# Where a two-layer transformer kernel puts its modulation work, how its first stream's norm is split, and how its first two query heads are ordered

## The chip, the cores and the metric

The kernel runs on one core of one Trainium2 chip. The metric is the device time of one execution in microseconds (us), lower is better. The core has TensorE (PE in the profile; PEld are its weight loads), VectorE (DVE), ScalarE (ACT), GpSimd (POOL) and SyncE (SP, which here only issues DMAs). Each engine works through its own queue in order; they wait for one another through semaphores. The instruction order on each engine comes from the framework's planner, which places instructions by their dependences and by where the program issues them.

## The reference

Two streams of 256 tokens with 1024 features go through two layers: `lat` (the first stream, s = 0) and `cx`, the context (the second stream, s = 1). Each layer has a feed-forward net (SwiGLU, 2816 hidden features), a mixer and a second feed-forward net. Each of the three steps is preceded by an RMS norm that is modulated, and its result is added through a gate. The nine shift, scale and gate vectors of a layer come from a product of the condition with a 1024 x 9216 matrix.

```python
mod  = (silu(c) @ mod_w[i] + mod_b[i]).reshape(bsz, 3, 3, 1, 1024)
modc = (silu(c_ctx) @ mod_w[i] + mod_b[i]).reshape(3, 3, 1024)
_modulate(t, g, shift, scale) = rms(t) * g * (1 + scale) + shift
lat = lat + 0.5 * mod[:,0,2] * swiglu(modulate(lat, norm_g[i,0], mod[:,0,0], mod[:,0,1]))   # cx likewise
lat = lat + mod[:,1,2] * mixer(...)       # layer 0: gated 3-tap convolution; layer 1: attention, 8 query and 2 key heads
lat = lat + 0.5 * mod[:,2,2] * swiglu(modulate(lat, ...))   # cx likewise, in layer 0 only
```

Everything is float32; only `lat` is returned.

## The kernel before

**Arithmetic.** x is held transposed: eight tiles (k = 0 to 7) of 128 features x 512 columns, the first stream in columns 0 to 255, the second in 256 to 511. A float32 product is made of three matmuls on a high and a low part (`mm3`, lines 137 to 139): w high by m high, w high by m low, w low by m high. Every weight and every operand is split first: ScalarE makes the high part (`split`, line 108, wh, bh, gh), VectorE the low part as the difference (line 109, wl, bl, gl).

**Stages in order.** `ffn(0, 0)`, the convolution's input product, its output product `cw_out`, `ffn(0, 1)`, `ffn(1, 0)`, attention, `wo` and `ffn(1, 1)` (that last one has only the first stream left). A feed-forward net for both streams runs in three parts (THIRDS: 8, 7 and 7 tiles of hidden features). Each part is a stretch of *block pairs* and then a *product* (`project`) of the hidden tiles with w2 into x.

**Block pairs.** `Pair` (lines 693 to 777) computes gate and up of one hidden tile in the seven-product form for 2 x 2 blocks: sums of weight blocks (VectorE lines 728 and 736, GpSimd line 706 with an adding DMA at 709, and a split w4h on ScalarE at 113 with w4l behind it) and then products in two PSUM tiles p and q (`head`, `five`, `six`, `seven`, `four`). Line 759 copies q into gm on ScalarE between two products into q.

**Products.** `project` (lines 586 to 645) makes eight output tiles m. The first `nf` (two or three) are interleaved with the end of the pairs; then one tile after another. `finish` adds the gated result into x on VectorE (line 569). A product that is followed by a norm (the third of a net, and `cw_out`) has `late` = 2: its tiles 6 and 7 are done at the end per stream and per half of the hidden tiles, so that the norm of the first stream can begin while the second stream's tiles are still computed.

**Norm.** `square_add` squares x on ScalarE (line 264, sq) and adds up on VectorE (line 272, acc). `rms_sum` adds over partitions with one-column matmuls (line 281, ss), takes the root on ScalarE (line 287) and the reciprocal on VectorE (line 290); `rms_all` spreads it with matmuls (line 299). Then each k tile is scaled on VectorE (line 311, t), shifted on ScalarE into the high part and made into the low part on VectorE. `Plain` does the latter two per k tile (lines 321 and 322). `Blocks` keeps four k tiles of one K half in one 128 x 1024 tile per stream, and a raw copy (line 405, hr). With `fine` it writes the high part (line 400, bh) and the low part (line 401, bl) per k tile; without, one `split` of the whole 128 x 1024 tile follows (lines 407, 108, 109). `fine` is set for the first stream's first K half only.

**Modulation.** After the first two chunks, the modulation's product isn't done on TensorE. One *unit* is a multiply-and-reduce on VectorE of 128 rows of the matrix with the condition (line 179, junk, and a readout of the accumulator into mod). The matrix rows (in_modT) come through SP's queue into the same ring of eight raw buffers (wr) as the weights. Units are handed out by `tick(n)`: it adds n to what is owed and issues whole units. There are ticks after product tiles (line 622 for the first nf, line 633 for the others up to tile 5, or up to tile 4 where late = 2), one of 0.5 in each pair (line 841), 5 for each tile of the convolution, and a few in attention. `ev` is the number for a product's tile: one value for the first two products of a net, one for its third. With `at` (late = 2 and m > 2) the units are placed behind that tile's line-569 instruction. `gate_of` and `mod_ready` issue at once whatever unit is needed and still missing.

**Attention.** `q_proj(p)` makes two query heads (i = 0, 1) side by side in one PSUM tile, all k of the first and then all k of the second. `sums` squares them on ScalarE and adds up over partitions; `rotate` scales them on ScalarE and applies the rotary tables.

Of the kernel before, what the change touches and what calls it, by code (L numbers as in the profile page):

```python
# [12 lines left out]
AF = mybir.ActivationFunctionType  # L13
# [34 lines left out]
def hybrid_kernel(ctx: ExitStack, tc: tile.TileContext, a: dict, out: bass.AP):  # L48
# [471 lines left out]
    def tail_norm(l, j, h):  # L520

        box = {}

        def tail(m, c0, c1):
            square_add(m, c0, c1)
            if m == KT - 1:
                if not box:
                    box["A"] = scale_of(l, j)
                    box["B"] = mod_ready(l, 3 * j)
                s = c0 // S  # L530

                def inv():
                    return rms_inv(s, (accs[s], accs[s, "last"]))

                def rest(part, ri):

                    if isinstance(h, Blocks):
                        h.block(s, part, box["A"], box["B"], ri, fine=s == 0 and part == 0)
                    else:
                        for k in range(4 * part, 4 * part + 4):  # L540
                            norm_k(s, k, h, box["A"], box["B"], ri)

                def both_parts():
                    ri = inv()
                    for part in range(2):
                        rest(part, ri)

                if s == 0:
                    keep = []

                    def one():
                        keep.append(inv())
                        rest(0, keep[0])

                    pending.append(one)
                    pending.append(lambda: rest(1, keep[0]))
                else:
                    flush()
                    pending.append(both_parts)

        return tail
# [24 lines left out]
    def project(ws, src, nk, gate, tail, tot, late, ev, between=()):  # L586

        def products(ps, w, ks, c0, c1, wide=True):
            ms = [src(k, c0, c1) for k in ks]
            if wide and len(ms[0]) == 3:
                return mm_wide(ps, [w(k) for k in ks], ms, ks[0] == 0, ks[-1] == nk - 1)
            for k, m in zip(ks, ms):
                mm3(ps[:, : c1 - c0], w(k), m[:2], k == 0, k == nk - 1)

        nf = 3 if between else 2  # L600
        ahead = {}

        def get(m):
            for i in range(m, min(m + 3, KT)):
                if i not in ahead:
                    ahead[i] = ws(i)
            return ahead[m]

        w2 = [get(m) for m in range(nf)]
        p2 = [psum("py") for _ in range(nf)]  # L610
        cut = nk - 2 if between else nk - 1
        for i in range(nf):
            products(p2[i], w2[i], range(cut), 0, tot)
            if i < len(between):
                between[i]()
        if between:
            for i in range(nf):
                products(p2[i], w2[i], (nk - 2,), 0, tot)
        for i in range(nf):
            products(p2[i], w2[i], (nk - 1,), 0, tot)  # L620
            finish(i, p2[i], 0, tot, gate, tail, len(src(0, 0, tot)) == 3)
            tick(ev)

        for m in range(nf, KT - late):
            if tail and tot == S and m == KT - 2:
                ready()
            w = get(m)
            ps = psum("py")
            wide = len(src(0, 0, tot)) == 3 and m < KT - 1
            products(ps, w, range(nk), 0, tot, wide)  # L630
            ins = finish(m, ps, 0, tot, gate, tail, wide)
            if m < (5 if late else 6):
                tick(ev, ins if late and m > 2 else None)
        if late:

            wl = [get(m) for m in (6, 7)]
            if tail:
                ready()
            for s in range(2):
                for i in range(2):  # L640
                    ps = psum("py")
                    products(ps, wl[i], range(nk // 2), s * S, s * S + S)
                    flush(1)
                    products(ps, wl[i], range(nk // 2, nk), s * S, s * S + S)
                    finish(6 + i, ps, s * S, s * S + S, gate, tail)
# [133 lines left out]
    def ffn(l, b, h, tot, gate, tail, gs=(), ev=(0, 0), z=None):  # L779
        gs = list(gs)  # L780
        i0 = 0
        for t, n in enumerate(THIRDS):
            between = ()
            if tot == T2:
# [23 lines left out]
                for i in range(len(gs), n):  # L808
                    if t == 0 and not heads and i in AS_IS[l, b]:
                        w = load_w(a["w13"][l, b, i])  # L810
                        pp = psum("pg"), psum("pu")
                        if prev:
                            prev.seven()
                        if "T1" not in h.t:
                            with tc.issue_after(rows["W1"]):
                                h.sums()
                        w13_mm(pp, w, h, range(4), 0, T2)
                        if prev:
                            gs.append(new_pair("g"))
                            prev.four(gs[-1])  # L820
                            prev = None
                        w13_mm(pp, w, h, range(4, KT), 0, T2)
                        gs.append(new_pair("g"))
                        tick(3, w13_post(pp, gs[-1], 0, T2))
                        continue
                    if heads:
                        pr = heads.pop(0)
                    else:
                        pr = Pair(a["w13"][l, b, i0 + i], h)
                        pr.sums(0)  # L830
                        pr.sums(1)
                        pr.head()
                    pr.five()
                    if prev:
                        prev.seven()
                    pr.six()
                    if prev:
                        gs.append(new_pair("g"))
                        prev.four(gs[-1])
                    prev = pr  # L840
                    tick(0.5)

                def last():
                    gs.append(new_pair("g"))
# [231 lines left out]


    hn = Plain()
    ffn(0, 0, h, T2, gate_of(0, 0), tail_norm(0, 1, hn), gs0, (2.9, 2.4))
    h = hn  # L1080

    zs = []
# [37 lines left out]
    def by_pairs(key, box=None):  # L1120
# [10 lines left out]
    hn = Blocks()  # L1131
    project(
        by_pairs("cw_out"), lambda k, c0, c1: (zs[k][0][:, c0:c1], zs[k][1][:, c0:c1]), KT,
        gate_of(0, 1), tail_norm(0, 2, hn), T2, 2, 1.8,
    )
    h = hn
    hn = Blocks()
    ffn(0, 1, h, T2, gate_of(0, 2), tail_norm(1, 0, hn), (), (2.7, 2))
    h = hn


    hn = Plain()
    ffn(1, 0, h, T2, gate_of(1, 0), tail_norm(1, 1, hn), (), (2.5, 1.6))
    h = hn
    ap = ctx.enter_context(tc.tile_pool(name="ap", bufs=2))

# [2 lines left out]

    def sums(ps, c):  # L1150
        sq = tp.tile([P, T2], F32, name=nm("sq"), tag="gm", bufs=3)
        nc.scalar.activation(out=sq, in_=ps, func=AF.Square)
        for i in range(4):
            nc.tensor.matmul(
                pqs[:, c + i : c + i + 1], sq[:, i * P : i * P + P], ones[:, 0:1],
                start=True, stop=True,
            )

    def rotate(ps, gain, n):

        kn = hot("kn", F32)[:, :T2]
        nc.scalar.activation(out=kn, in_=ps, func=AF.Identity, scale=gain)
        rt = tp.tile([P, T2], F32, name=nm("rt"), tag="sg", bufs=3)
        for o in range(0, P, 32):
            nc.scalar.dma_start(rt[o : o + 32, : n * S], kn[o ^ 32 : (o ^ 32) + 32, : n * S])
        v3 = lambda t: t[:, : n * S].rearrange("p (i t) -> p i t", i=n)
        sb = sinT.unsqueeze(1).to_broadcast([P, n, S])
        cb = cosT.unsqueeze(1).to_broadcast([P, n, S])
        nc.vector.tensor_tensor(out=v3(rt), in0=v3(rt), in1=sb, op=ALU.mult)
        kc = tp.tile([P, T2], F32, name=nm("kc"), tag="gm", bufs=3)  # L1170
        nc.vector.tensor_tensor(out=v3(kc), in0=v3(kn), in1=cb, op=ALU.mult)
        nc.vector.tensor_tensor(
            out=kn[:, : n * S], in0=kc[:, : n * S], in1=rt[:, : n * S], op=ALU.add
        )
        return kn

    def q_proj(p):
        wq = load_w(a["wq"][p])
        ps = psum("pq")
        for i in range(2):  # L1180
            for k in range(KT):
                mm3(
                    ps[:, i * S : i * S + S], wq(k * 256 + i * P), pick(h, k, 0, S),
                    k == 0, k == KT - 1,
                )
        return ps

    qs, krs = [], []

# [6 lines left out]
    def k_proj(kv):  # L1196
        ps = psum("pk")
        for k in range(KT):
            mm3(ps, wk(k * 256 + kv * P), pick(h, k, 0, T2), k == 0, k == KT - 1)
        return ps  # L1200

    def k_rope(kv, ps):
        sums(ps, 16 + 4 * kv)
# [272 lines left out]
```

## Time and profile before

| | |
|---|---|
| median of 3 runs | 1571.19 us (1570.63 to 1572.66) |
| profiled execution | 1571.39 us |
| its span, first to last instruction | 1569.6 us |
| mean granted TensorE clock | 0.998 |
| PE busy | 1554.6 us (99%) |
| DVE busy | 1284.9 us (82%) |
| ACT busy | 779.2 us (50%) |
| POOL busy | 224.4 us (14%) |

The profile is that of one execution; times count from the start of its span. A row of a timeline has start, duration, engine, line, operation, what is written and read, and in brackets the idle time ahead of it with what ended it. A row of waits has the waiting engine and what it waited for, then the total, the number of times and the longest. Consecutive PE rows overlap: matmuls are pipelined, so the distance between starts tells the pace, not the duration. The stages lie at: first net 48 to 382 us (its products at 114 to 161, 229 to 270 and 339 to 382), convolution to 516, `cw_out` to 564, `ffn(0, 1)` to 917, `ffn(1, 0)` to 1267, attention to 1358, the rest to 1569.6.

### The profile page before, as it was taken

What the parts mean: (1) busy time and instruction counts of PE and PEld (TensorE: products, weight loads), DVE (VectorE), ACT (ScalarE), POOL (GpSimd) and SP (SyncE); (2) the same over time, 40 slices, a digit from 0 to 9 for tenths busy, and PEclk for the clock granted to TensorE, in tenths of its full rate; (3) what the DMA queues carried; (4) which work ended last, traced back from release to release, by engine and by line L of the source; (5) the groups of instructions that cost most, each with busy time, mean ns of one, the idle gap of its engine ahead of it and who ended that gap; (6) DMA issues with size and microseconds to landing.
All of it is one profiled execution on the core that took longest, in us unless ns stands there. A gap on an engine that the chain in (4) does not pass through costs nothing.

```text
span 1569.6 us, 26355 instructions
## 1 busy us (share of the span) xinstructions
PE 1554.6 (99%) x10282; PEld 1423.0 (91%) x10282; DVE 1284.9 (82%) x2023; ACT 779.2 (50%) x1289; POOL 224.4 (14%) x188
## 2 busy tenths in 40 slices
PE   9999999999999999999999999999999999999999
PEld 7898998999888899989989899989999899898888
DVE  5789789779997688987987798987978797887676
ACT  5642552644423366436346476436345355674553
POOL 0013203200000022041131021031041002300000
PEclk9999999999999999999999999999999999999999
DMA  9567657554564434664664544664765664356562
GB/s 371 190 181 205 146 155 201 120 174 147 181 223 161 129 100 121 195 175 106 199 168 125 166 119 122 195 171 112 254 170 156 195 197 144 97 192 210 171 199 74
DMA packets 88253, 263.53 MB, mean 168 GB/s; under 512 B 10816, under 2 KB 12608, under 8 KB 88128
## 3 DMA queue, kind: packets, MB, share of 16 engines
q1 hardware_dynamic: 69408, 230.72, 45.3%
q0 software_dynamic: 16128, 29.37, 11.1%
q10 hardware_dynamic: 2592, 1.76, 0.4%
q8 instruction: 80, 1.31, 0.3%
q14 instruction: 45, 0.37, 0.1%
HBM read 259.45 MB, written 1.05 MB: 166 GB/s over the span
## 4 chain that ended last, share of the span: by engine, by line
PE 83%; DVE 8%; DMA 4%; issue 2%; ACT 2%; ACTq 0%; POOL 0%; POOLq 0%; DVEq 0%; SPq 0%
PE py L137 7%; PE py L138 7%; PE py L139 7%; PE p L137 6%; PE p L138 6%; PE p L139 6%; PE q L137 5%; PE q L139 5%; PE q L138 5%; DVE junk L179 2%; PE py L145 2%; PE pg L145 2%; PE pu L145 2%; DVE wl L109 2%; DMA wr<-in_w 1%
## 5 line engine op out<-in xcount | busy, mean ns | idle before, releaser
L108 ACT ACTIVATE wh<-wr 128x1024 fp32r<-128x1024 f32 (+2 forms) x446 | 394.6, 913 | 339.3 <-PE py L138 127.1
L109 DVE TENSOR_TENSOR wl<-wr,wh 128x1024 fp32r<-128x1024 f32 (+2 forms) x446 | 458.0, 1051 | 106.5 <-ACT wh L108 84.8
L179 DVE CUSTOM_DVE_ANT_0 junk<-wr,scbc,modb 128x1024 bf16<-128x1024 f32 x222 | 286.0, 1288 | 26.0 <-DMA wr<-in_modT 23.9
L137 PE MATMUL py<-gh,wh 128*128 128x512 f32 (+1 forms) x570 | 213.4, 374 | 0.0
L138 PE MATMUL py<-gl,wh 128*128 128x512 f32 (+1 forms) x570 | 213.3, 374 | 0.0
L139 PE MATMUL py<-gh,wl 128*128 128x512 f32 (+1 forms) x570 | 212.9, 373 | 0.0
L706 POOL TENSOR_SCALAR wr<-wr 128x512 f32<-128x512 f32 x56 | 100.5, 1795 | 714.6 <-DMA wr<-in_w 495.9
L569 DVE SCALAR_TENSOR_TENSOR x<-py,mod,x 128x256 f32<-128x256 f32 x213 | 94.2, 478 | 41.4 <-PE py L139 30.2
L138 PE MATMUL p<-tl,wh 128*128 128x256 f32 x448 | 126.8, 283 | 0.0
L139 PE MATMUL p<-th,wl 128*128 128x256 f32 x448 | 126.8, 283 | 0.0
L137 PE MATMUL p<-th,wh 128*128 128x256 f32 x448 | 126.7, 283 | 0.0
L139 PEld LDWEIGHTS py<-gh,wl 128*128 128x128 f32 x570 | 107.3, 188 | 19.2
L137 PEld LDWEIGHTS py<-gh,wh 128*128 128x128 f32 x570 | 107.4, 188 | 18.3
L138 PEld LDWEIGHTS py<-gl,wh 128*128 128x128 f32 x570 | 107.4, 188 | 18.1
L115 POOL DMA_DIRECT2D w4l<-in_w x56 | 52.0, 929 | 280.8 <-ACT w4l L114 204.9
L137 PE MATMUL q<-bh,wh 128*128 128x256 f32 x320 | 90.8, 284 | 0.7 <-ACT gm L759 0.7
L139 PE MATMUL q<-bh,wl 128*128 128x256 f32 x320 | 90.7, 283 | 0.2 <-DVE wl L109 0.2
L138 PE MATMUL q<-bl,wh 128*128 128x256 f32 x320 | 90.5, 283 | 0.0
L137 PEld LDWEIGHTS p<-th,wh 128*128 128x128 f32 x448 | 86.0, 192 | 0.4
L138 PEld LDWEIGHTS p<-tl,wh 128*128 128x128 f32 x448 | 86.0, 192 | 0.3
L139 PEld LDWEIGHTS p<-th,wl 128*128 128x128 f32 x448 | 86.0, 192 | 0.0
L766 ACT ACTIVATE sg<-sg 128x512 f32<-128x512 f32 x56 | 35.4, 632 | 86.7 <-DVE sg L765 86.6
(304 smaller groups left out, 4067.6 us busy)
## 6 DMA issues: line engine op xcount, KB each, us to landing
wr<-in_modT SPq DMA_DIRECT2D x126, 512.0 KB, 4.9
wr<-in_w SPq DMA_DIRECT2D x120, 512.0 KB, 4.5
wr<-in_w2b SPq DMA_DIRECT2D x64, 448.0 KB, 4.0
wr<-in_w2a SPq DMA_DIRECT2D x32, 512.0 KB, 4.9
wr<-in_w SPq DMA_DIRECT2D x56, 256.0 KB, 4.0
wr<-in_w POOLq DMA_DIRECT2D x56, 256.0 KB, 4.9
w4l<-in_w POOLq DMA_DIRECT2D x56, 256.0 KB, 5.9
pm<-in_mod SPq DMA_DIRECT2D x16, 512.0 KB, 10.2
```

Of the source, the lines that this page charges most:

```text
L108: nc.scalar.activation(out=hi, in_=src, func=AF.Copy)
L109: return nc.vector.tensor_tensor(out=lo, in0=src, in1=hi.bitcast(F32), op=ALU.subtract)
L115: nc.gpsimd.dma_start(out=lo, in_=src, accum_op=ALU.add)
L137: nc.tensor.matmul(ps, wh, mh, start=first, stop=False, **kw)
L138: nc.tensor.matmul(ps, wh, ml, start=False, stop=False, **kw)
L139: nc.tensor.matmul(ps, wl, mh, start=False, stop=last, **kw)
L145: nc.tensor.matmul(ps, w[0], m[2], start=first and n == 0, stop=False)
L179: nc.vector.tensor_tensor_reduce(out=junk, in0=raw[j], in1=scbc[:, v, :], scale=0.5 if ch in (2, 8) else 1.0, scalar=modb[:, l, col : col ...
L569: ins = nc.vector.scalar_tensor_tensor(out=x[:, m, s * S : s * S + S], in0=ps[:, o : o + S], scalar=g[:, m, s : s + 1], in1=x[:, m, s * S ...
L706: nc.gpsimd.tensor_scalar(out=r1[:, :T2], in0=r2[:, :T2], scalar1=-1.0, scalar2=None, op0=ALU.mult)
L766: nc.scalar.activation(out=self.sg, in_=self.sg, func=AF.Silu)
```

## The change

There are four edits.

- `fine` is set for both K halves of the first stream. The second K half's single split of 128 x 1024 (one ScalarE, one VectorE instruction) becomes four of each with 128 x 256. This concerns the norms ahead of `ffn(0, 1)` and `ffn(1, 0)`.
- In a product the tick of the last tile that had one is dropped: tile 5 has none any more where late = 0, tile 4 where late = 2. The numbers `ev` of the remaining ticks go up.
- In the block pairs a tick of 0.8 stands behind every pair but the first of a stretch, in place of 0.5 behind each.
- `q_proj(0)` uses two PSUM tiles, one for each head, and goes through k with both heads at each k. `sums` and `rotate` take a list of tiles; for pair 0 each of their ScalarE instructions becomes two of 256 columns.

```diff
-                        h.block(s, part, box["A"], box["B"], ri, fine=s == 0 and part == 0)
+                        h.block(s, part, box["A"], box["B"], ri, fine=s == 0)
...
-            if m < (5 if late else 6):
-                tick(ev, ins if late and m > 2 else None)
+            if m < 5 - late // 2:
+                tick(ev, ins if late and m == 3 else None)
...
-                    tick(0.5)
+                    if i:
+                        tick(0.8)
...
-    ffn(0, 0, h, T2, gate_of(0, 0), tail_norm(0, 1, hn), gs0, (2.9, 2.4))
+    ffn(0, 0, h, T2, gate_of(0, 0), tail_norm(0, 1, hn), gs0, (3, 2.7))
...
     project(
         by_pairs("cw_out"), lambda k, c0, c1: (zs[k][0][:, c0:c1], zs[k][1][:, c0:c1]), KT,
-        gate_of(0, 1), tail_norm(0, 2, hn), T2, 2, 1.8,
+        gate_of(0, 1), tail_norm(0, 2, hn), T2, 2, 2.2,
     )
...
-    ffn(0, 1, h, T2, gate_of(0, 2), tail_norm(1, 0, hn), (), (2.7, 2))
+    ffn(0, 1, h, T2, gate_of(0, 2), tail_norm(1, 0, hn), (), (2.8, 2.4))
...
-    ffn(1, 0, h, T2, gate_of(1, 0), tail_norm(1, 1, hn), (), (2.5, 1.6))
+    ffn(1, 0, h, T2, gate_of(1, 0), tail_norm(1, 1, hn), (), (2.8, 2))
...
     def sums(ps, c):
         sq = tp.tile([P, T2], F32, name=nm("sq"), tag="gm", bufs=3)
-        nc.scalar.activation(out=sq, in_=ps, func=AF.Square)
+        for o, p in enumerate(ps):
+            n = p.shape[1]
+            nc.scalar.activation(out=sq[:, o * n : o * n + n], in_=p, func=AF.Square)
...
-        nc.scalar.activation(out=kn, in_=ps, func=AF.Identity, scale=gain)
+        for o, p in enumerate(ps):
+            m = p.shape[1]
+            nc.scalar.activation(
+                out=kn[:, o * m : o * m + m], in_=p, func=AF.Identity, scale=gain
+            )
...
     def q_proj(p):
         wq = load_w(a["wq"][p])
-        ps = psum("pq")
-        for i in range(2):
-            for k in range(KT):
-                mm3(
-                    ps[:, i * S : i * S + S], wq(k * 256 + i * P), pick(h, k, 0, S),
-                    k == 0, k == KT - 1,
-                )
-        return ps
+        if p == 0:
+
+            ps = [psum("pq")[:, :S] for _ in range(2)]
+            order = [(i, k) for k in range(KT) for i in range(2)]
+        else:
+            ps = psum("pq")
+            ps = [ps[:, :S], ps[:, S:], ps]
+            order = [(i, k) for i in range(2) for k in range(KT)]
+        for i, k in order:
+            mm3(ps[i], wq(k * 256 + i * P), pick(h, k, 0, S), k == 0, k == KT - 1)
+        return ps[2:] or ps
```

More of the change, by code (lines that the diff above doesn't have):

```diff
@@ L1199, in k_proj @@
             mm3(ps, wk(k * 256 + kv * P), pick(h, k, 0, T2), k == 0, k == KT - 1)
-        return ps
+        return [ps]
     def k_rope(kv, ps):
```

## The prediction

> **What bounds the kernel now.** I read the page's busy shares first, then its slices, then the chain that ended last.
>
> ```profile
> span 1569.6 us, 26355 instructions
> PE 1554.6 (99%) x10282; PEld 1423.0 (91%) x10282; DVE 1284.9 (82%) x2023; ACT 779.2 (50%) x1289; POOL 224.4 (14%) x188
> ...
> PEclk9999999999999999999999999999999999999999
> ...
> PE 83%; DVE 8%; DMA 4%; issue 2%; ACT 2%; ACTq 0%; POOL 0%; POOLq 0%; DVEq 0%; SPq 0%
> ```
>
> TensorE is busy for 99% of the span at nearly full clock, and 83% of the chain is its own work. The change removes no matmul, so it can win only what TensorE loses between matmuls; 1569.6 - 1554.6 = 15.0 us is idle in all. The view of TensorE's waits says for whom it stood still:
>
> ```profile
> PE q L137 <- ACT gm L759: 1.9, 2, 1.2
> PE ss L281 <- ACT sq L264: 1.7, 2, 1.0
> ...
> PE pg L138 <- DVE bl L109: 1.0, 1, 1.0
> PE ss L281 <- DVE acc L272: 0.7, 2, 0.4
> ...
> PE ss L299 <- DVE ri L290: 0.6, 1, 0.6
> ...
> PE pq L137 <- ACT hh L321: 0.4, 1, 0.4
> ...
> PE pv L137 <- ACT hh L321: 0.3, 1, 0.3
> PE pq L138 <- DVE hl L322: 0.3, 1, 0.3
> ```
>
> All of these stand at seams, where one product ends and the next stage begins; the waits inside attention and the start-up are not touched by the edits. They add up to 6.9 us. The tables by stretch show which engine is short there (columns: length, then busy time of PE, PEld, DVE, ACT, POOL, then clock; the last row counts the modulation reductions of line 179 alone):
>
> ```profile
> 228.88:269.91 41.03, 41.03 (x195) 34.42 (x193) 40.10 (x65) 11.92 (x16) 9.47 (x8) 1.00 0.72 213
> 269.91:338.70 68.79, 67.58 (x563) 67.38 (x562) 55.24 (x76) 40.49 (x69) 14.40 (x13) 1.00 0.56 139
> ...
> 559.10:562.60 3.50, 3.50 (x19) 3.50 (x18) 2.35 (x7) 1.68 (x5) 1.93 (x2) 0.51 0.93 193
> ...
> 871.00:917.00 46.00, 44.83 (x261) 39.56 (x260) 35.60 (x67) 20.27 (x32) 7.00 (x7) 1.00 0.56 167
> ...
> 1260.00:1273.00 13.00, 12.07 (x92) 11.14 (x92) 11.96 (x27) 6.83 (x14) 0.00 (x0) 1.00 0.53 183
> ```
> ```profile
> 269.91:338.70 68.79, 6.37 (x10) 1.00 0.56 139
> ```
>
> VectorE is 98% busy in a product (40.10 of 41.03 us) without stopping TensorE, and 80% busy in the block pairs behind it (55.24 of 68.79). What it has not finished when the product ends is what TensorE waits for. One row more: the clock is 0.51 for the one stretch from 559.10.
>
> **The change, part by part.** Durations are those of the profiled execution: 1571.39 us, of which 1569.6 are the span and 1.8 lie around it; it is 0.2 above the median of the runs, 1571.19.
>
> *Ticks off the last tiles (line 632), higher rates, and 0.8 a pair instead of 0.5 (line 841).* In the first ffn a product that took six ticks of 2.9 (17.4 units) takes five of 3 (15 units), so the last tick's three units no longer stand behind tile 5; pairs get six ticks of 0.8 (4.8) instead of seven of 0.5 (3.5). The seam at 275 us:
>
> ```profile
> 275.42 0.28 PE L138 MATMUL p<-tl,wh 128*128 128x256 f32 x1
> 275.54 0.28 PE L139 MATMUL p<-th,wl 128*128 128x256 f32 x1
> 277.03 0.39 PE L137 MATMUL q<-hh,wh 128*128 128x256 f32 x1 [1.21 <-ACT gm L759]
> ```
> ```profile
> 269.85 1.27 DVE L179 CUSTOM_DVE_ANT_0 junk<-wr,scbc,modb 128x1024 bf16<-128x1024 f32 x1
> 271.06 0.08 DVE L179 DVE_READ_ACCUMULATOR2_ANT mod<- 128x1 f32 x1
> ...
> 274.81 0.68 DVE L728 TENSOR_TENSOR wr<-wr 128x512 f32<-128x512 f32 x1
> ```
> ```profile
> 275.66 1.06 ACT L108 ACTIVATE wh<-wr 128x1024 fp32r<-128x1024 f32 x1 [3.75 <-DVE wr L728]
> ```
>
> The matmul waits for the copy gm (line 759), which on ScalarE is queued behind the split wh, which waits for VectorE's line 728. A unit is 1.27 + 0.08 = 1.35 us of VectorE; three gone put line 728 up to 4.0 us earlier, more than the wait. Matmuls start 1.49 us apart here and 0.12 apart before (275.42, 275.54), so the loss is 1.37: a listed wait costs 0.16 more than its entry. The row of waits has two such (1.9 us), so 2.2 us go if all goes; nothing goes if line 728's weights land late instead. I take -1.9, nearer the first, since ScalarE and VectorE, not a DMA, are named in these rows.
>
> The work comes back in the pairs: 1.3 units on average, at most 2, or 2.7 us of VectorE, so 57.9 of 68.79 us (84%). What hides it: 13.5 us of VectorE idleness in that stretch, 1.9 for each of seven pairs. I take 0; the product before it, 98% busy with TensorE full, is the nearest row. Without that cover it is the slow rival below. The modulation loads (512 KB each) move past pair loads on SP's queue too; POOL's loads keep their order. They share the ring of eight raw buffers, so a load can wait there, and what is behind it on SP waits with it.
>
> *No modulation behind the late tiles at 556 us (cw_out; m < 4 instead of m < 5).*
>
> ```profile
> 556.61 0.28 PE L138 MATMUL py<-zl,wh 128*128 128x256 f32 x1
> 557.86 0.38 PE L281 MATMUL ss<-ones,sq 128*128 128x1 f32 x2 [0.97 <-ACT sq L264]
> ...
> 561.22 0.41 PE L137 MATMUL py<-zh,wh 128*128 128x256 f32 x1
> 561.43 0.41 PE L138 MATMUL py<-zl,wh 128*128 128x256 f32 x1
> ```
> ```profile
> 555.67 1.28 DVE L179 CUSTOM_DVE_ANT_0 junk<-wr,scbc,modb 128x1024 bf16<-128x1024 f32 x1
> ...
> 556.88 0.48 DVE L569 SCALAR_TENSOR_TENSOR x<-py,mod,x 128x256 f32<-128x256 f32 x1
> ```
> ```profile
> 554.36 0.63 ACT L113 ACTIVATE w4h<-wr 128x512 fp32r<-128x512 f32 x1 [2.19 <-DMA wr<-in_w]
> ```
>
> The last square waits for x of tile 7, which waited behind a unit (1.28 us from 555.67) on VectorE. That unit is gone in the new order, so the stall of 0.97 + 0.16 = 1.1 goes. Right behind it the clock halves: matmuls 0.21 us apart instead of 0.12. About 15 of the 19 in that stretch are full ones, so 15 x 0.09 = 1.35 us. The other long stalls (1.21 at 275, 0.96 at 924) show no such drop, so that the stall was its cause is likely, not certain. I take both, -2.5; with the ri wait (0.6 + 0.16) it could be -3.2, and 0 if w4h's late load (ScalarE idle 2.19 us for it) still holds the square up.
>
> [...]
>
> *First stream's norm by k tile in the second K half (line 538), with the last tick gone there too.* The seam from 909 to 925:
>
> ```profile
> 924.14 0.28 PE L137 MATMUL pu<-bh,wh 128*128 128x256 f32 x1
> 925.38 0.39 PE L138 MATMUL pg<-bl,wh 128*128 128x256 f32 x1 [0.96 <-DVE bl L109]
> ```
> ```profile
> 915.02 1.26 DVE L311 SCALAR_TENSOR_TENSOR t<-x,A,ss 128x256 f32<-128x256 f32 x3
> 916.25 0.48 DVE L401 SCALAR_TENSOR_TENSOR bl<-t,mod,bh 128x256 fp32r<-128x256 f32 x1
> ...
> 924.11 1.22 DVE L109 TENSOR_TENSOR bl<-hr,bh 128x1024 fp32r<-128x1024 f32 x1
> ```
> ```profile
> 918.09 0.50 ACT L400 ACTIVATE bh<-t,mod 128x256 fp32r<-128x256 f32 x1
> 918.49 0.50 ACT L405 ACTIVATE hr<-t,mod 128x256 f32<-128x256 f32 x1
> ```
>
> One bl of 1.22 us that must be whole becomes four of 0.48, each needed at its own k; TensorE now waits at each, with pu of the same k queued behind. On VectorE four cost 1.92 - 1.22 = 0.7 more, on ScalarE about as much (four of 0.50 for one of 1.06 us: 0.9); ScalarE is busy 20.27 of 46 us there, so this hides. What is late next is VectorE's supply: 0.42 for t and 0.48 for bl, 0.9 us per k tile, against six matmuls of 0.12 = 0.72 on TensorE. Over three tiles that leaves 3 x 0.18 = 0.5 of the wait of 0.96 + 0.16. The waits ss for sq (1.7 - 0.97 = 0.7) and for acc (0.4) stand behind units of the last tick, which go; with 0.16 each they are 1.4, and I take 0.9 for what another load on ScalarE may keep. Together -(0.6 + 0.9) = -1.5; the ends are -2.5 and +0.7 (the added VectorE work, uncovered). The same edit before the first ffn's second half has no listed wait for bl: 0.
>
> *First query heads side by side, and the seams to conv (381 us) and attention (1262 us).* In pair 0 each k tile now feeds two heads, so TensorE takes 0.72 instead of 0.36 us per k while the norm supplies one in about 0.9; the listed waits pq are 0.4 + 0.3, with 0.16 each 1.0, and the table has 13.00 - 12.07 = 0.93 idle. Two 256-column copies replace one of 512 in sums and rotate, ScalarE only (6.83 of 13 busy). I take -0.7, ends -1.0 and +0.4. At conv pv's wait (0.3 + 0.16) loses the units ahead of its norm: -0.4, ends -0.5 and 0.
>
> Sum: -1.9 - 2.5 - 1.5 - 0.7 - 0.4 + 0 = -7.0, so 1571.39 - 7.0 = 1564.4 us. All gains at their ends: -2.2 - 3.2 - 2.5 - 1.0 - 0.5 = -9.4, 1562.0. All at the other end: 0 + 0 + 0.7 + 0.4 + 0 = +1.1, 1572.5.
>
> **The rivals.**
>
> *The waits are handed on* (1569.7 us). ScalarE's strict order keeps the squares behind w4h's load and the weights behind line 728 land late; only half of the waits of q for gm (1.1) and the 0.6 of bl go: -1.7, 1569.7. For it: 2.19 us of ScalarE idleness for a DMA at 552 to 554. Against: the rows nearest the stalls name VectorE's units.
>
> *More goes than the waits show* (1560). Of the 15.0 us idle the rows quoted above are 6.9; the other 8.1 hold start-up and attention, but also stops at the seams too short to be listed, which a VectorE that is ahead would take too. I put this end at the -9.4 and 2 of the 8.1, so -11.4.
>
> *Slower: pairs starve* (1576). A unit whose load is late stops VectorE in order.
>
> ```profile
> DVE junk L179 <- DMA wr<-in_modT: 23.9, 19, 3.8
> ```
>
> It waited 19 times, up to 3.8 us. In a product this is covered by nothing being urgent; in a pair VectorE's room is 1.9 us, and the pair's own splits stand behind. If in the six pair stages after a first product one such wait exceeds the room by its whole 3.8 - 1.9 = 1.9 us, it costs 11.4, and with the gains 1571.39 - 7.0 + 11.4 = 1575.8. It decides from four such waits on (7.6 us). For it: loads sharing one ring with the pair's. Against: pairs already carry five units in 68.79 us and show no wait behind them but the seam's.
>
> *The clock drop stays, or falls elsewhere*, the change doing the rest, because a stop of 1 us is not what halves it: 1564.4 + 1.35 = 1565.8, in the forecast's own range. Against it speaks the place, right behind the stop; for it that two other stops did nothing. [...]
>
> **How the numbers follow.** A chance of 0.50 for the forecast (1561.5 to 1567.5), 0.15 of it for the clock drop that stays, 0.12 for more than the waits show, 0.22 for waits handed on, 0.16 for starving pairs. 0.2% (3.1 us) is about what a measurement of this kernel can tell from no change. Faster takes the forecast and the second case, 0.62; within 0.2% the handed-on waits, 0.22; slower 0.16. The range, 1560 to 1574, leaves out the far half of the slow case and a little of the fast one.
>
> **What the profile after would show.** Right: no row of q waiting for gm at the first seam; no wait of ss for sq near 557, and no stretch of clock near 0.5 there; four bl of 0.48 us in place of 1.22 near 923, with a wait under 0.6; line 179 at about 15 units instead of 17 in a product and about 5 to 6 in a pair stage, TensorE as busy as 67.58 of 68.79 or more there. Wrong: new rows of p or q waiting for wl or wh inside pair stages, modulation waiting longer for its loads than 23.9 us, or the squares still behind w4h.

## The result and the profile after

The changed kernel is slower by a little: median 1573.61 us over 22 executions (1569.73 to 1579.83) against 1570.68 us for the kernel before (1567.11 to 1572.66); the ratio is 1.0023 with a 95% interval of [1.0013, 1.0032]. The forecast was 1564.4 us and faster.

The profiled execution took 1570.84 us, with a span of 1569.1 us and a granted clock of 0.998; it is one of the quicker ones. Over the 22 executions the clock lay between 0.992 and 0.999, mean 0.9964; before's, in the four sets taken for the experiments, had means of 0.9980 to 0.9985. In the profile before, one window at half clock lasts 3.4 us (matmul starts are 0.21 us apart from 559.1 to 562.5). Such a window counts 3.4 x 0.5 / 1570 = 0.0011 of the mean clock, so by this estimate the changed kernel runs through one to two of them more. A line through its 22 points gives 1.2 us for each 0.001: some 2 of the 2.9 us between the medians go along with the clock.

The page after, its busy shares:

```profile
span 1569.1 us, 26378 instructions
PE 1552.7 (99%) x10282; PEld 1421.2 (91%) x10282; DVE 1282.2 (82%) x2029; ACT 776.3 (49%) x1297; POOL 223.0 (14%) x188
```

TensorE idles 1569.1 - 1552.7 = 16.4 us where it idled 15.0. The total hardly moved; the places did. TensorE's waits after:

```profile
PE ss L281 <- DVE acc L272: 3.8, 3, 1.9
PE pq L139 <- DVE wl L109: 3.0, 1, 3.0
PE ss L299 <- DVE ri L290: 1.2, 2, 0.6
...
PE q L137 <- ACT wh L108: 0.4, 1, 0.4
...
PE pg L138 <- DVE bl L401: 0.2, 1, 0.2
```

The waits of q for gm, of ss for sq, of pv and pq for hh are gone, and bl's fell from 1.0 to 0.2. In their place stand acc (0.7 before, 3.8 now) and one of 3.0 us for wl in attention, at a place that had none. Of acc's waits one is at the start-up, which the edits leave alone: 0.32 us of the 0.7 and 1.91 us of the 3.8 (0.2 to 1.9 us over the profiles of all runs here). The two others are new in size: 0.76 at 905 us and 1.10 at 1257. q's wait for wh, 0.39 us, is new, too; it is at 591 us, in the first block pair of `ffn(0, 1)`. TensorE's timeline at the stop in attention, and the clock behind it (after's table by stretch):

```profile
1296.86 1.05 PE L1249 MATMUL kri<-ident,rq 128*128 128x128 f32 x8
1300.93 0.57 PE L139 MATMUL pq<-hh,wl 128*128 128x256 f32 x1 [3.02 <-DVE wl L109]
...
1301.52 0.41 PE L138 MATMUL pq<-hl,wh 128*128 128x256 f32 x1
1301.73 0.41 PE L139 MATMUL pq<-hh,wl 128*128 128x256 f32 x1
```
```profile
1300.80:1304.40 3.60, 3.47 (x16) 3.47 (x17) 3.60 (x6) 0.00 (x0) 0.00 (x0) 0.53 0.75 198
```

The fourth query pair's product stops at its third matmul. Matmul starts are 0.21 us apart behind the stop instead of 0.12; the 14 matmuls until 1304.3 take some 14 x 0.09 = 1.3 us more. What VectorE did meanwhile (timeline after):

```profile
1295.55 0.08 DVE L179 DVE_READ_ACCUMULATOR2_ANT mod<- 128x1 f32 x1
1299.32 0.42 DVE L1176 TENSOR_TENSOR rt<-rt,sinT 128x256 f32<-128x256 f32 x1 [3.68 <-DMA rt<-kn]
1299.66 1.22 DVE L109 TENSOR_TENSOR wl<-wr,wh 128x1024 fp32r<-128x1024 f32 x1
```

It did nothing for 3.68 us: the rotation rt of the second key head waits for its DMAs, and the low part wl that TensorE wants is queued behind it. Before, that low part stood ahead of the rotation (timeline before):

```profile
1299.35 1.22 DVE L109 TENSOR_TENSOR wl<-wr,wh 128x1024 fp32r<-128x1024 f32 x1
...
1303.69 0.43 DVE L1169 TENSOR_TENSOR rt<-rt,sinT 128x256 f32<-128x256 f32 x1 [0.77 <-DMA rt<-kn]
```

### The profile page after: what moved, and what is told of

Its sections match the earlier page's. It is cut to its first block, busy times and chain, and to the rows that moved or that the text cites. A ratio compares the mean times of both kernels' runs of the same rounds, so it can differ in the third digit from the quotient of the medians.

```text
span 1569.1 us, 26378 instructions
## 1 busy us (share of the span) xinstructions
PE 1552.7 (99%) x10282; PEld 1421.2 (91%) x10282; DVE 1282.2 (82%) x2029; ACT 776.3 (49%) x1297; POOL 223.0 (14%) x188
## 4 chain that ended last, share of the span: by engine, by line
PE 89%; DVE 5%; DMA 3%; ACT 2%; issue 1%; ACTq 0%; POOLq 0%; POOL 0%; DVEq 0%; SPq 0%
PE py L138 8%; PE py L137 8%; PE py L139 8%; PE p L137 7%; PE p L138 7%; PE p L139 7%; PE q L139 5%; PE q L137 5%; PE q L138 5%; PE py L145 2%; PE pu L145 2%; PE pg L145 2%; DVE wl L109 1%; PE pv L138 1%; PE pv L137 1%; PE pv L139 1%
## 5 line engine op out<-in xcount | busy, mean ns | idle before, releaser
L179 DVE CUSTOM_DVE_ANT_0 junk<-wr,scbc,modb 128x1024 bf16<-128x1024 f32 x220 | 283.6, 1289 | 37.2 <-DMA wr<-in_modT 35.4
L113 ACT ACTIVATE w4h<-wr 128x512 fp32r<-128x512 f32 x56 | 35.2, 628 | 86.7 <-DMA wr<-in_w 47.9
```

Source lines behind the costliest of these rows:

```text
L113: nc.scalar.activation(out=hi, in_=raw, func=AF.Copy)
L179: nc.vector.tensor_tensor_reduce(out=junk, in0=raw[j], in1=scbc[:, v, :], scale=0.5 if ch in (2, 8) else 1.0, scalar=modb[:, l, col : col ...
```

## The experiments

The first four runs take the change apart.

**The heads one after another again, all else as changed.** The edit gives `q_proj`, `sums` and `rotate` back their old form (of the edit, the loop alone):

```diff
-        if p == 0:
...
-            ps = [psum("pq")[:, :S] for _ in range(2)]
-            order = [(i, k) for k in range(KT) for i in range(2)]
...
+        for i in range(2):
+            for k in range(KT):
...
```

> The changed kernel with the first query heads one after the other again. Theory A (the new order in attention: the low part of the third query weights stands behind a rotation that waits for its DMA; TensorE stops 3.2 us at 1297 us and the clock halves behind it): both go, so the seams' gain of about 7 us shows; about 1564.5, ratio to before 0.9955 to 0.9965. Theory B (the changed kernel's short stops at 566, 590, 904, 1256 halve the clock in one execution and not in another, and that is the loss): only the 3.2 us go, 1569.5 to 1571, and the granted clock of its executions still spreads from 0.992 to 0.999. Theory C (the added modulation in the pairs costs): as B, with TensorE waits in pair stages.

Measured: 1571.58 us, ratio 1.001 [1.0001, 1.0019]. The stop at 1297 us is gone, as A and B had it, but the seams' gain of A doesn't show, and the time is 0.6 us above the range of B: the last seam got worse (2.27 us of waiting for acc at 1258 us), and the clock of the 12 executions lay between 0.996 and 1.0, not down to 0.992.

```profile
PE ss L281 <- DVE acc L272: 4.1, 3, 2.3
...
PE pq L138 <- DVE hl L322: 0.7, 4, 0.2
```

**The side-by-side heads alone on the kernel before.**

> The kernel before with the first query heads side by side and nothing else. Theory A: the attention order is disturbed here too, a stop of 2 to 4 us there and often a halved clock window (1.5 us) behind it: 1572 to 1576. Theories B and C: no more than 1 us from before.

Measured: 1569.17 us, ratio 0.9993 [0.9984, 1.0002]: no cost and no stop in attention. Theory A as stated falls: this edit by itself does not make the stop. Here the first low part of the fourth pair (1298.55) stands ahead of the rotation (1301.68, 0.60 us of waiting); only together with the moved ticks does the planner lay them the other way round. (Whether it needs the norm by k tile for that, too, no run shows; heads and norm together, in the run ticks_back below, don't have the stop.)

**The moved ticks alone.**

> The kernel before with the ticks and rates moved and nothing else. Theory A: the seams at 275, 556 and 808 us gain: 1564 to 1567. Theory B: no gain or slower, clock spread down to 0.993. Theory C: slower, 1572 or more, with waits of p or q for wl or wh in the pairs.

Measured: 1579.38 us (6 executions), ratio 1.0061 [1.0048, 1.0073]. A's gain is refuted. B's "no gain or slower" holds, with a clock of 0.994 to 0.997, and so does C's time, but hardly C's cause: in the pairs q waits for wh only twice, 0.39 us each. Most of the large stops lie at the norm seams. TensorE's timeline and the clock there:

```profile
911.37 0.38 PE L281 MATMUL ss<-ones,acc 128*128 128x1 f32 x2 [1.49 <-DVE acc L272]
...
924.97 0.39 PE L137 MATMUL pg<-bh,wh 128*128 128x256 f32 x1 [1.30 <-ACT bh L108]
926.23 0.58 PE L138 MATMUL pg<-bl,wh 128*128 128x256 f32 x1 [0.76 <-DVE bl L109]
```
```profile
567.00:570.50 3.50, 3.50 (x19) 3.50 (x18) 0.70 (x1) 0.00 (x0) 1.75 (x2) 0.52 0.37 126
912.00:919.00 7.00, 7.00 (x35) 7.00 (x35) 3.57 (x11) 2.98 (x7) 3.33 (x3) 0.52 0.84 154
926.00:931.50 5.50, 5.28 (x24) 5.28 (x25) 0.25 (x2) 0.00 (x0) 2.37 (x2) 0.50 0.28 88
```

The norm's second K half, split as a whole, is now what TensorE runs into (1.30 + 0.76 us), and 16 us of the span run at half clock (the three stretches of the second table). The difference to no_side_by_side (which has the same ticks and the norm by k tile) is 1579.38 - 1571.58 = 7.8 us: with the ticks moved, the norm by k tile is worth that; without, nothing:

**The norm by k tile alone.**

> The kernel before with the first stream's second K half normed by k tile and nothing else. All theories: the wait of pg for bl at 924 us (0.96 us) falls to under 0.5 and nothing else moves: 1570 to 1571, not to be told from before.

Measured: 1569.99 us, ratio 1.0001 [0.9993, 1.001], as expected in time.

The kernels before, heads alone and norm alone issue the same instructions in the same order in the whole first net. Yet q's waits for gm there came to 1.21 us (before), 0.92 (heads alone) and 0.48 + 0.23 (norm alone). So a single profile carries half a microsecond of chance in one net.

The next four go at the two orders which the profile after shows.

**The low part ahead of the rotation.** The fourth pair's weights are loaded ahead of `k_rope(1)`, whose rt is queued behind their wl:

```diff
+    w3 = load_w(a["wq"][3])
     k_rope(1, pk[1])          # its rt inside tc.issue_after(last wl)
     inv_rms(16, 24)
-    pq.append(q_proj(3))
+    pq.append(q_proj(3, w3))
```

> The changed kernel; in attention the low part of the fourth query pair's weights is queued on VectorE ahead of the second key head's rotation. Theory D (the stop of 3.2 us at 1297 us is a place in VectorE's queue: the weights' low part behind a rotation that waits for its DMA): the stop goes and with it the halved clock window behind it; 3.2 to 4.8 us below the changed kernel, 1568.8 to 1570.4, ratio to before 0.999 to 1.000. Rival (the stop is one of the profiled execution, or another takes its place): within 1.5 us of the changed kernel, 1572 to 1574.

Measured: 1568.10 us, ratio 0.998 [0.9972, 0.9989]; once more, in another session, 1567.82 us and 0.9982 [0.9969, 0.9994]. In the two profiles the orders of all engines differ between 1289 and 1320 us only, so nothing else is at work. This one place is worth 0.0043 of 1570 = 6.7 us by the ratios (5.5 by the medians, each against its own runs of before), and it turns the change from slower into faster by a little. No wait of pq for wl is left, and the mean clock of the executions is 0.9982 instead of 0.9964. In the profiles the stretch from the first query product to the first scores shrinks from 53.08 to 48.29 us, by 4.8. What the gain has beyond that may lie in the clock of the other executions, which no profile shows.

**The squares ahead of the next net's w4h.** In the profile after, ScalarE waits 1.87 us for weights, then loads the root's table, then squares tile 6:

```profile
902.76 0.63 ACT L113 ACTIVATE w4h<-wr 128x512 fp32r<-128x512 f32 x1 [1.87 <-DMA wr<-in_w]
903.41 1.28 ACT L584 ACT_TABLE_LOAD   x1
904.71 0.20 ACT L584 ACTIVATE ready<-acc 128x1 f32<-128x1 f32 x1
904.82 0.40 ACT L264 ACTIVATE sq<-x 128x256 f32<-128x256 f32 x1
```

The edit queues w4h behind the first stream's last square:

```diff
...
+                with tc.issue_after(squared[0]):
+                    split_far(*self.w["A22"], r2[:, :T2], self.src[:, 1024 : 1024 + T2])
```

> The changed kernel; at the seams to the two nets in block form ScalarE's two w4h splits are queued behind the first stream's last square. Theory E (ScalarE's order hands the wait on: w4h waits 1.9 us for its weights at 901 us, the load of the root's table and the square of tile 6 stand behind it, and ss waits 0.76 us for acc): that wait of ss at 905 us falls below 0.3, fewer halved clock windows follow; 1 to 2.5 us below the changed kernel, 1571 to 1572.5. Rival (VectorE's units keep acc late): the wait stays over 0.6 and the time within 0.7 us of the changed kernel.

Measured: 1572.20 us, ratio 1.0012 [1.0001, 1.0022]. The wait of ss for acc at 905 us is gone (the square now starts at 902.58), so ScalarE's order was what held acc up there. But two waits of pg for bl (0.29 and 0.35) and other short stops came in its place, and though the median is inside E's range, the time can't be told from the changed kernel's: the two intervals overlap.

**Both orders.**

> The two former edits together. Theories D and E: their gains add, 4 to 7 us below the changed kernel, 1566.5 to 1569.5, ratio to before 0.997 to 0.9995. If the loss sits in the clock alone: 1570 or more, with a mean granted clock as low as the changed kernel's 0.996.

Measured: 1568.32 us, ratio 0.9987 [0.9977, 0.9997]: the second order adds nothing to the first that the intervals could tell.

**The ticks of before, with the other two edits.**

> The changed kernel with the ticks and rates of before (norm by k tile and heads side by side stay). If the moved ticks are what costs: at least 3 us below the changed kernel, 1568 to 1570, ratio to before 0.9985 to 1.0. If the three edits only hurt together in attention: the stop of 3 us in attention is gone, too, but the seams lose their 7 us again: 1573 or more.

Measured: 1569.33 us, ratio 0.999 [0.9979, 1.0]. This is in the range of the first expectation and looks as if the ticks cost 4.3 us. But this kernel doesn't have the stop in attention, so it compares the ticks and the order in attention at once.

What was left was the last seam, from `ffn(1, 0)` to attention, where the kernels with moved ticks stop at ss. VectorE's timeline in third_weights_first (its lines 181 and 571 are 179 and 569 of the kernel before):

```profile
1251.81 1.28 DVE L181 CUSTOM_DVE_ANT_0 junk<-wr,scbc,modb 128x1024 bf16<-128x1024 f32 x1 [2.52 <-DMA wr<-in_modT]
1253.02 0.08 DVE L181 DVE_READ_ACCUMULATOR2_ANT mod<- 128x1 f32 x1
1253.02 0.87 DVE L571 SCALAR_TENSOR_TENSOR x<-py,mod,x 128x256 f32<-128x256 f32 x2
...
1256.00 1.27 DVE L181 CUSTOM_DVE_ANT_0 junk<-wr,scbc,modb 128x1024 bf16<-128x1024 f32 x1
...
1257.60 0.41 DVE L274 TENSOR_TENSOR acc<-acc,sq 128x256 f32<-128x256 f32 x1
```
```profile
1250.00:1258.10 8.10, 6.55 (x55) 6.34 (x53) 6.21 (x12) 3.79 (x6) 0.00 (x0) 1.00 0.73 252
1259.00:1262.40 3.40, 3.40 (x18) 3.40 (x18) 1.86 (x4) 1.38 (x3) 0.00 (x0) 0.50 0.52 166
```

A unit waits 2.52 us for its load, ahead of x of tile 5, and another stands ahead of acc; TensorE idles 1.55 us and a halved window follows (0.50 from 1259.0 to 1262.4 us). Theory F of the next run is that these units are not those of the product's ticks, but belong to attention's first ticks, and that the planner lays them into the product's end.

**Those units behind attention's weights.**

```diff
-    tick(1)          # after k_proj(0), k_proj(1); likewise tick(2) after q_proj(2)
+    tick(1, low[0])  # low[0]: the last wl so far
```

> The kernel of the run third_weights_first, with the modulation units of attention's first three ticks queued on VectorE behind the low parts of the weights loaded last. Theory F (units of attention's ticks were laid into the end of the last product before it; the stop of ss for acc at 1256 us, 1.7 us, and the halved clock behind it come from such a unit that waits 2.5 us for its load): the stop falls under 0.5 and the halved window at 1260 goes, 2 to 3.5 us below that run: 1564.5 to 1566.5, ratio to before 0.9955 to 0.997. Rival (the stop is ScalarE's table load ahead of the square): the stop stays over 1 us and the time within 1 us of that run, ratio 0.998.

Measured: 1568.27 us, ratio 0.9986 [0.9973, 0.9999]. The stop of ss at 1256 and the halved window are gone, as F said (ss waits for acc twice, 2.5 us in all, where it did three times, 3.2 us; the profiled execution's mean clock is 0.999 instead of 0.997), but the time missed its range: it didn't move. The units now stand ahead of the scores. The same stretch, this run and then third_weights_first:

```profile
1308.00:1327.00 19.00, 17.17 (x111) 14.06 (x110) 15.12 (x37) 10.72 (x24) 7.80 (x6) 1.00 0.27 80
```
```profile
1308.00:1327.00 19.00, 19.00 (x140) 17.79 (x140) 15.50 (x39) 11.75 (x25) 8.00 (x6) 1.00 0.25 78
```

**The same with the ticks of before**, so that the order in attention is nearly the same in both and the ticks alone differ.

> The same with the ticks and rates of before, so that the order in attention is the same and the ticks alone differ. If the moved ticks gain at the seams as predicted: 4 to 6 us above the run attention_units_behind, 1569 to 1571. If they gain nothing once attention is out of the way: within 1.5 us of it.

Measured: 1572.34 us, ratio 1.0011 [1.0001, 1.0021]. The moved ticks are worth 0.9986 against 1.0011, 3.9 us by the ratios and 4.1 by the medians: the gain at the seams is there. Its size is less sure than that. The intervals allow some 2.5 us either way, and in the two profiles 1.2 us of the difference come in the scores, where VectorE has one modulation unit at another place, and 1.3 at the start-up; from the first net to the end of `ffn(1, 0)` it is 2.9 us.

**The four units handed out in the convolution.**

```diff
-        tick(5)
+        tick(5.5)
...
-    tick(1)   # both, and the tick(2) after q_proj(2)
```

> The kernel of the run third_weights_first; the four units of attention's first three ticks are handed out in the convolution instead (5.5 a tile in place of 5), and those ticks go. Theory G (what the run attention_units_behind won at 1256 us it gave back because the same units then stood ahead of the scores on VectorE): both the stop of ss for acc at 1256 us and the stops of psc and pt at 1309 to 1326 us (3 us) stay away, the convolution (VectorE 89% busy) takes the units without a stop of TensorE: 2 to 4 us below third_weights_first, 1564 to 1566. Rival (the time is set elsewhere, the seam's loss moves on to t and hl of attention's norm): within 1 us of third_weights_first.

Measured: 1565.26 us (7 executions), ratio 0.9963 [0.9948, 0.9978], as G had it: faster than both kernels. Neither the stop at 1256 us nor those in the scores are there, and the convolution takes the units without a stop of TensorE (130.98 of 131.00 us):

```profile
382.00:513.00 131.00, 130.98 (x639) 110.82 (x639) 120.90 (x184) 44.94 (x60) 0.00 (x0) 1.00 0.58 189
1250.00:1258.00 8.00, 8.00 (x69) 7.94 (x68) 4.02 (x12) 3.48 (x7) 0.00 (x0) 1.00 0.39 131
```

**The run beside it** is the kernel of third_weights_first again.

> The kernel of third_weights_first once more beside the one above, on the same chip, to have their difference from one set of runs: ratio to before 0.997 to 0.999, with the stop of ss for acc at 1256 us of 1 us or more.

Measured: 1567.82 us, ratio 0.9982 [0.9969, 0.9994], within what was expected.

## Why the prediction was wrong, and where it was right

The step that failed is the first one of the reading: "the waits inside attention and the start-up are not touched by the edits". The part on the heads priced two more ScalarE instructions and the two listed waits of pq, -0.7, and did not ask what else the planner would lay differently. With the ticks and the heads both changed, it put a rotation that waits for a DMA ahead of a low part that TensorE needs. That one place cost 3.0 us of waiting and a halved window (0.53 from 1300.8 to 1304.4 us), and the runs put its whole worth at 6.7 us by the ratios, nearly the -7.0 of the sum. The reading had followed VectorE's order at the seams, and not through attention. That 1573.61 still lies inside the range of 1560 to 1574 is luck: the slow end stood there for pairs that starve, and they did not.

The sum had no term either for what the moved ticks bring to the end of `ffn(1, 0)`, where it counted a gain. With both places put right, in four_units_to_conv, the time is 0.9963 of before, some 5.8 us less: the way of the forecast, and most of its size.

The profiles size the parts by stage, as distance between the first matmuls of the stages (us; one execution each):

| | first net | convolution | `cw_out` | `ffn(0, 1)` | `ffn(1, 0)` | attention up to the scores |
|---|---|---|---|---|---|---|
| before | 283.84 | 133.56 | 48.35 | 352.24 | 350.07 | 50.43 |
| after | 281.68 | 133.43 | 45.60 | 351.31 | 352.29 | 53.08 |
| third_weights_first | 281.80 | 133.43 | 45.59 | 352.77 | 352.27 | 48.29 |
| four_units_to_conv | 281.69 | 133.44 | 45.59 | 351.55 | 350.02 | 48.23 |

*Ticks, seam at 275 and its like (-1.9).* The waits of q for gm are gone in the profile after, where pairs run without a stop:

```profile
270.00:338.00 68.00, 68.00 (x567) 67.92 (x566) 56.38 (x77) 39.88 (x69) 10.52 (x11) 1.00 0.54 136
```

But one profile doesn't settle this step: kernels with the old ticks show 0.7 to 1.9 us for that wait, those with the moved ones from none (after) to 2.1 (ticks_alone). The means of the five and the nine profiles are 1.1 and 0.5 us. The first net as a whole, with its seam to the convolution, is 1.2 us shorter in the mean with the moved ticks (282.1 against 283.3), where the sum had -1.9 (the seam at 809 us included) and -0.4: the kernel before was profiled in an execution with long waits.

*cw_out at 556 (-2.5).* The wait went as said: no wait of ss for sq, and in the profile after the clock is full there (1.00 from 554 to 572 us). The ri wait stayed, at 0.6, as assumed. But the term is too large. The table gives 2.75 us from before to after, yet the four other kernels with the old ticks take 46.2 to 46.5 us there, against 45.5 to 45.6 with the moved ticks: 0.6 to 1.0 us. That the halved window which the sum priced at 1.35 us was a chance of the one profiled execution is an estimate from these times; one of the four, ticks_back, had a mean clock of 1.0 in its profiled execution.

*Norm by k tile (-1.5).* The wait for bl fell to 0.2, better than the 0.5 left over. But ss waits for acc at 905, 0.76 us, for the reason that the rival of the handed-on waits named: w4h's load on ScalarE, with the table load between. In the five other profiles with both edits and w4h in this place the wait is 0.7 to 1.4 us, and behind that of no_side_by_side (1.42 us at 904) the clock is 0.62 from 905.0 to 909.5 us, so of the 0.9 for ss little or nothing came. By itself this edit gave nothing; its 7.8 us show only once the ticks let the norm come early. The steps were priced one by one, and these two are not independent.

*Heads and attention's seam (-0.7).* The waits of pq went, but ss for acc (1.10) and ri (0.58) came, from units which attention's own ticks issue. The edit to the product's ticks cannot keep those away. By the table `ffn(1, 0)` is 2.2 us longer for it, and the two runs that put these units elsewhere (attention_units_behind, 349.47, and four_units_to_conv) have it back. The side-by-side heads themselves gave more than -0.7 where the order is right: 49.04 us up to the scores in side_by_side_alone against 50.43.

*The pairs (0).* Right but for q's 0.39 us at 591, which fine_alone and ticks_back have with the old ticks, too. The slow rival is refuted in its place: 6 units instead of 5 in the stretch (the row of line 179 alone, two instructions a unit), and TensorE full.

```profile
267.00:336.00 69.00, 7.72 (x12) 1.00 0.53 131
```

Its mechanism did occur, though, in a product's end: modulation waited 35.4 us for its loads in all instead of 23.9, and at 1251 and 1259 us (2.08 and 1.92) it cost. So all three signs of being wrong that the prediction named came: q's wait for wh, the longer waits for modulation loads, and a square behind w4h (at 904.82). Its signs of being right at 275, 557 and 923 us came beside them, and none of the signs looked into attention.

*The clock.* The prediction took one halved window as gone with its stop. That window went; others came behind the new stops. The stop's length alone does not tell where (3.02 us, then 0.53; 1.55, then 0.50; 0.97, then 0.51; but 1.10 and 0.76 in the profile after and 1.21 in the profile before, then 1.00). What does was not shown: no run here varied a stop alone.

*One reading of a row.* The wait of ss for acc, 0.7 us in two, was counted among the seams; 0.32 of it is at the start-up. The sum used the other 0.4 alone, so nothing hangs on it.

What the sum had for the ticks, -1.9 - 2.5 - 0.9 - 0.4 = -5.7, stands against 3.9 to 4.1 us measured for them in like surroundings (2.9 at the seams of the two profiles): the gain is there, smaller than forecast, and it was given back in attention and at its seam.

## What to carry to other kernels

When a planner lays out the queues, an edit's price includes every queue whose order moves, also at a place that the edit doesn't name: compare the orders over the whole kernel, and look for an instruction that waits for a DMA in front of one that the bound engine needs. Work that fills gaps lands in the gap that looks free, so tie it down where a tight chain follows, or hand it out where the other engine has slack to the end, as the convolution had. Edits at one seam are priced together: what the second is worth can depend wholly on the first. A wait or a halved window that one profile shows once is not priced in full before a second profile has it.

## What the runs showed of the hardware

TensorE's clock fell to half behind some stops and stayed full behind others. It was 0.51 from 559.1 to 562.5 us, 3.4 us, in the kernel before, behind a stop of 0.97 us; 0.53 from 1300.8 to 1304.4 us in the changed kernel, behind the stop of 3.02 us in attention; 0.50 from 1259.0 to 1262.4 us in third_weights_first, behind one of 1.55 us. It stayed at 1.00 behind the stops of 1.21 us at 277 us and of 0.96 us at 925 us in the kernel before, and in the changed kernel behind those of 1.10 us at 1257 us and of 0.76 us at 905 us:

```profile
1255.50:1258.60 3.10, 2.00 (x17) 1.79 (x16) 1.85 (x4) 0.95 (x4) 0.00 (x0) 1.00 0.70 222
1258.60:1262.00 3.40, 2.82 (x23) 2.61 (x23) 2.31 (x6) 1.78 (x4) 0.00 (x0) 1.00 0.51 165
903.00:912.00 9.00, 8.24 (x70) 8.03 (x69) 6.10 (x16) 6.60 (x14) 5.90 (x5) 1.00 0.89 189
```

Executions of one and the same kernel differ with the clock, too: the changed kernel's ran from 1569.73 us at a clock of 0.999 to 1579.83 at 0.992.
